# Mixer AB: ten taps of the Conformer convolution on TensorE instead of eight, fed by one more weight unit

## The chip, the cores and the metric

The kernel runs on one core of a Trainium2 chip. The metric is the device time of one execution in microseconds. The time before is 1874.81 us, the median of 3 runs (1874.71 to 1875.68).

## What is computed

The reference is a two-layer decoder trunk on a residual stream x of 512 tokens by 1024 features, in fp32. Each layer is a half-step SwiGLU FFN, a token mixer and another FFN, and every sub-layer is normalised before and after. The mixer of layer 0 is "AB". Its input projection gives four groups of 512 columns. Two of them feed the recurrent half (A), the other two the convolution half (B):

```python
z = h @ w_in
a_gate, a_x, b_val, b_gate = jnp.split(z, [W_A, 2 * W_A, 2 * W_A + W_B], axis=-1)
a_x = _causal_dwconv(a_x, a_conv_w, a_conv_b)                  # 4 taps
y_a = _rg_lru(a_x, a_gate_w, a_gate_b, a_lam) * jax.nn.gelu(a_gate)
v = b_val * jax.nn.sigmoid(b_gate)
v = _causal_dwconv(v, b_conv_w, b_conv_b)                      # 31 taps, one weight per channel and tap
v = layernorm of v over each of 8 groups of 64 channels
y_b = jax.nn.silu(v)
return jnp.concatenate([y_a, y_b], axis=-1) @ w_out
```

The change concerns the 31 taps of B's convolution: tap s adds v, shifted by s tokens and multiplied by one weight per channel, to the result.

## The kernel before

**Layout and precision.** Activations lie feature-major: a tile is 128 features by 512 tokens. Every fp32 matrix product is made from three TensorE passes over split operands (a rounded part and the rest, for weights and for activations): `mm3` (line 292) issues weight-high times data-high, weight-low times data-high and weight-high times data-low (lines 294 to 296).

**Phases.** FFN, mixer AB, FFN, FFN, mixer C, FFN follow each other, and the head of a phase overlaps the tail of the one before. During the first FFN a list of background jobs is run between its matmuls (`run_bg`, line 204): adaLN products, and for mixer AB `early` (line 683), which loads every weight unit of the mixer once, makes its low part (`split_w`, lines 280 and 281) and stores that to DRAM in `lows`.

**Mixer AB** (`rest`, line 931). The order of TensorE's units is written out in `ORDER` (line 31): "v t0 g x0 t1 x1 s0 t2 x2 s1 t3 x3 s2 a0 s3 a1 a2 a3". Here v and g are the last value and gate units of B, xj the inputs of A's recurrence, aj A's gate, sj the small gate products of the recurrence (lines 863 and 864, plain fp32), and tj the convolution taps of channel tile j. Then the output projection follows.

**The taps of tile j** go to three engines. TensorE takes the even shifts 0, 2, ..., 14 (NPE = 8) in `conv_pe` (line 759): each tap is a diagonal 128 by 128 weight and one `mm3` over 512 - 2i columns, all accumulated in one PSUM bank. Shift 1 is part of ScalarE's start value for GpSimd. `taps` (line 767) deals out the 22 other shifts: 11 (NPOOL) to GpSimd, for each of which ScalarE writes the product (line 784) and GpSimd adds it (line 785), and 11 to VectorE, which adds them into the PSUM bank that TensorE left (line 797). At line 802 VectorE joins both sums. Then `norm_b` (line 805) runs a chain between three engines: centring matmul (807), ScalarE (811, 813), group sums on TensorE (817), the reciprocal root on VectorE (325 to 335) and its copy (824), broadcast on TensorE (828), VectorE (833), ScalarE (836, 837), VectorE (839), ScalarE (842), VectorE (844).

**What sets the order of issue.** In this phase the instruction order of TensorE, ScalarE, VectorE and GpSimd is fixed by an issue clock kept in Python (`Flow`, line 226). Every `mm3` advances it by 3 times its columns over 2400. The side chains are generators that issue their next instruction once the clock has gone on by a constant: W_TAP = 0.9 after each VectorE tap, W_POOL = 1.404 after each GpSimd tap, W_N[0] = 0.5 between the last tap and line 802, W_N[1] = 4.0 between line 802 and the centring matmul. The queues of all engines are in order, so a side chain that runs late stops TensorE where its next matmul stands.

**Weight units.** `loads` (line 946) fetches each unit's 512 KB into one of four `raw` buffers (line 269, SyncE's queue), ScalarE makes the high part (line 953), and the low part comes back from `lows` (line 957). The units are taken in the order v, t0, g, x0 and so on. A unit tj holds eight diagonal weights, 1024 columns. v is split for the taps in `vsplit` (lines 926 and 928).

Of the kernel before, what the change touches and what calls it, by code (L numbers as in the profile page):

```python
# [7 lines left out]
F32 = mybir.dt.float32  # L8
F32R = mybir.dt.float32r
I32 = mybir.dt.int32  # L10
AF = mybir.ActivationFunctionType
# [3 lines left out]
P = 128  # L15
D = 1024
T = 512
KT = D // P
# [7 lines left out]

TMP, TMPH, CP = 4, 6, 2

NPE, NPOOL = 8, 11

ORDER = "v t0 g x0 t1 x1 s0 t2 x2 s1 t3 x3 s2 a0 s3 a1 a2 a3"
MANS = "PAVG"
# [50 lines left out]
def trunk_kernel(ctx: ExitStack, tc: tile.TileContext, a: dict, out: bass.AP):  # L83
    nc = tc.nc
    V, S, PE, G = nc.vector, nc.scalar, nc.tensor, nc.gpsimd
# [8 lines left out]
    def nm(base):  # L94
        uid[0] += 1
        return f"{base}_{uid[0]}"
# [9 lines left out]
    def t_hid(dt=F32):  # L106
        return sb.tile([P, T], dt, tag="hid", bufs=16, name=nm("hid"))
# [4 lines left out]
    def t_raw():  # L112
        return sb.tile([P, 1024], F32, tag="raw", bufs=4, name=nm("raw"))

    def t_mm(shape=(P, T)):
        return ps.tile(list(shape), F32, tag="mm", bufs=6, name=nm("mm"))
# [147 lines left out]
    def load_w(src, cols, eng=V):  # L264
        return split_w(fetch_w(src, cols), cols, eng)

    def fetch_w(src, cols):
        raw = t_raw()
        nc.sync.dma_start(raw[:, :cols], src)
        return raw  # L270

    def t_w():
        return (
            sb.tile([P, 1024], F32R, tag="wh", bufs=8, name=nm("wh")),
            sb.tile([P, 1024], F32R, tag="wl", bufs=8, name=nm("wl")),
        )
# [15 lines left out]
    def mm3(o, w, c0, hi, lo, start, stop, shared=False):  # L292
        wh, wl = w[0][:, c0 : c0 + P], w[1][:, c0 : c0 + P]
        PE.matmul(o, lhsT=wh, rhs=hi, start=start, stop=False, skip_group_check=shared)  # L294
        PE.matmul(o, lhsT=wl, rhs=hi, start=False, stop=False, skip_group_check=shared)  # L295
        PE.matmul(o, lhsT=wh, rhs=lo, start=False, stop=stop, skip_group_check=shared)  # L296
        flow.tick(3 * o.shape[1] / 2400)
# [176 lines left out]
    class PairHead(Ready):  # L474
# [6 lines left out]
        def fetch(self, k):  # L481
            self.raw[k] = fetch_w(self.src[k], 2 * self.n * P)
# [181 lines left out]
    lows = {}  # L664

    def low_jobs(srcs):
        def job(key, src, cols):
            wl = load_w(src, cols)[1]
            lows[key] = dram.tile([P, cols], F32, tag=nm("low"), name=nm("low"))
            later.append(lambda: nc.sync.dma_start(lows[key], wl.bitcast(F32)[:, :cols]))  # L670

        return [lambda v=v: job(*v) for v in srcs]


    class MixAB(Proj):
# [7 lines left out]
        def early(self):  # L683

            u = {"v": 0, "g": 1, **{f"x{j}": 2 + j for j in range(4)}, **{f"a{j}": 6 + j for j in range(4)}}
            src = lambda o: (a["ab_r"][u[o]], 1024) if o in u else (a["b_diag"][int(o[1])], NPE * P)
            units = [(o, *src(o)) for o in ORDER.split() if o[0] != "s"]
            return low_jobs(units + [(f"o{f}", self.wo[f], 1024) for f in range(KT)])

        def evac(self, j, val, gate, lo, hi):  # L690

# [67 lines left out]
        def conv_pe(self, j, w):  # L759
            vh, vl = self.vs[j][:, :T], self.vs[j][:, T:]  # L760
            o = t_mm()
            for i in range(NPE):
                c = T - 2 * i
                mm3(o[:, 2 * i :], w, i * P, vh[:, :c], vl[:, :c], i == 0, i == NPE - 1)
            self.ad[j] = o

        def taps(self):
# [163 lines left out]
        def rest(self):  # L931
# [3 lines left out]
            self.cv, self.ad, self.vs, self.x, self.y, self.sq = {}, {}, {}, {}, {}, set()  # L935

            r = lambda n: (a["ab_r"][n], 1024)
            d = lambda j: (a["b_diag"][j], NPE * P)
            unit_of = {"v": r(0), "g": r(1)}
            for j in range(4):  # L940
                unit_of[f"t{j}"], unit_of[f"x{j}"], unit_of[f"a{j}"] = d(j), r(2 + j), r(6 + j)
            order = ORDER.split()
            srcs = [(o, *unit_of[o]) for o in order if o in unit_of] + [(f"o{f}", self.wo[f], 1024) for f in range(KT)]
            ready = []

            def loads():
                while srcs:
                    while len(ready) > AHEAD:
                        yield 0.3
                    key, src, cols = srcs.pop(0)  # L950
                    raw = fetch_w(src, cols)
                    wh, wl = t_w()
                    S.activation(wh[:, :cols], raw[:, :cols], AF.Copy)
                    if len(ready) > 1:
                        yield 1.0
                    if key in lows:
                        nc.sync.dma_start(wl.bitcast(F32)[:, :cols], lows[key])
                    else:
                        V.tensor_tensor(
                            wl[:, :cols], raw[:, :cols], wh[:, :cols].bitcast(F32), op=SUB  # L960
                        )
                    ready.append((wh, wl))
                    if len(ready) > 1:
                        yield 1.0
# [4 lines left out]
            def wait(cond):  # L969
                while not cond():  # L970
                    flow.tick(0.2)

            def unit():
                wait(lambda: ready)
                return ready.pop(0)
# [5 lines left out]
                flow.start(self.gated(j, feat(None, unit())))  # L981

            def taps(j):
                wait(lambda: j in self.vs)
                self.conv_pe(j, unit())

            flow.tick(0)
# [281 lines left out]
    for n, ph in enumerate(phases):  # L1269
# [14 lines left out]
        with tc.manual_schedule(engines={nc.tensor.engine, nc.vector.engine}):  # L1284
            free = 8 - len(ph.wt)
            units = [] if last else list(range(KT))
# [128 lines left out]
```

## Time and profile before

| what | us |
|---|---|
| median of 3 runs | 1874.81 |
| the profiled execution, its own time | 1874.57 |
| its span, first to last instruction | 1872.4 |
| TensorE busy in the span | 1843.8 |
| VectorE busy | 1116.1 |
| ScalarE busy | 706.1 |
| GpSimd busy | 153.0 |

The span is what the instructions of the profiled execution cover; the remaining 2.17 us lie around it. Matmuls are pipelined, so that the busy time of a group of them counts overlaps twice; the start of the next one tells what one costs. The mixer's units v to a3 run from 429.46 to 543.54 us of the span.

### The profile page before, as it was taken

The page shows a single profiled execution, that of the slowest core. Times are in us where ns is not written, and L with a number is a line of the kernel's source. Part 1 is how long each engine was busy: PE and PEld are TensorE (multiplying, and loading weights), DVE is VectorE, ACT ScalarE, POOL GpSimd, SP SyncE. Part 2 cuts the span into 40 slices and gives each one's busy share as a digit, 9 for nine tenths or more (in the row PEclk, how much of TensorE's full clock was granted, in tenths as well). Part 3 has the DMA queues.
Part 4 walks back from the last instruction along what each step waited for, and adds up shares of the span by engine and source line. Part 5 has one row for each costly group of instructions (what it writes and reads, how often), then busy time and mean ns, then how long its engine had stood idle before and what let it go on. Part 6 is the DMA issues. An engine that isn't in the chain of part 4 may idle for free.

```text
span 1872.4 us, 25021 instructions
## 1 busy us (share of the span) xinstructions
PE 1843.8 (98%) x9636; PEld 1559.7 (83%) x9636; DVE 1116.1 (60%) x1967; ACT 706.1 (38%) x1058; POOL 153.0 (8%) x166
## 2 busy tenths in 40 slices
PE   9999999999799999999999999999999999999997
PEld 7788888998579888888898888888978998888887
DVE  7876767485856765455366665653675573344434
ACT  4444434246865433222234433232343342222221
POOL 0000000126512000000020000000300200000002
PEclk9999999999999999999999999999999999999999
DMA  8589889446355475564234996763433343334211
GB/s 330 183 306 309 317 315 315 131 163 222 135 203 169 163 272 190 162 222 153 92 119 167 318 310 217 278 237 103 158 101 119 119 127 112 118 94 134 90 45 46
DMA packets 103370, 344.76 MB, mean 184 GB/s; under 512 B 11473, under 2 KB 13649, under 8 KB 103250
## 3 DMA queue, kind: packets, MB, share of 16 engines
q1 hardware_dynamic: 103250, 343.16, 54.2%
q8 instruction: 76, 1.25, 0.3%
q14 instruction: 44, 0.36, 0.1%
HBM read 302.22 MB, written 40.89 MB: 183 GB/s over the span
## 4 chain that ended last, share of the span: by engine, by line
PE 92%; DVE 5%; ACT 2%; issue 1%; DMA 0%; POOL 0%; DVEq 0%; ACTq 0%; POOLq 0%
PE mm L296 29%; PE mm L294 29%; PE mm L295 29%; DVE ad L152 1%; PE st L345 1%; PE mm L1076 1%; PE mm L1078 1%; PE mm L1077 1%; PE st L355 1%; DVE mm L797 0%; PE mm L1129 0%; DVE y L408 0%; ACT tmp L1233 0%; ACT hh L1231 0%; DVE x L415 0%
## 5 line engine op out<-in xcount | busy, mean ns | idle before, releaser
L294 PE MATMUL mm<-hh,wh 128*128 128x512 f32 (+1 forms) x1728 | 641.7, 371 | 0.0
L296 PE MATMUL mm<-hl,wh 128*128 128x512 f32 (+1 forms) x1728 | 637.8, 369 | 0.1
L295 PE MATMUL mm<-hh,wl 128*128 128x512 f32 (+1 forms) x1728 | 636.3, 368 | 0.0
L280 ACT ACTIVATE wh<-raw 128x1024 fp32r<-128x1024 f32 (+2 forms) x324 | 328.1, 1016 | 528.4 <-PE mm L296 187.2
L281 DVE TENSOR_TENSOR wl<-raw,wh 128x1024 fp32r<-128x1024 f32 (+2 forms) x324 | 377.9, 1171 | 182.8 <-ACT wh L280 167.8
L296 PE MATMUL mm<-hid,wh 128*128 128x256 f32 (+1 forms) x1164 | 384.5, 330 | 0.0
L294 PE MATMUL mm<-hid,wh 128*128 128x256 f32 (+1 forms) x1164 | 384.0, 330 | 0.1
L295 PE MATMUL mm<-hid,wl 128*128 128x256 f32 (+1 forms) x1164 | 380.6, 327 | 0.0
L295 PEld LDWEIGHTS mm<-hh,wl 128*128 128x128 f32 x1728 | 325.3, 188 | 61.2 <-issue 1.7
L294 PEld LDWEIGHTS mm<-hh,wh 128*128 128x128 f32 x1728 | 325.0, 188 | 60.0 <-issue 2.0
L296 PEld LDWEIGHTS mm<-hl,wh 128*128 128x128 f32 x1728 | 325.0, 188 | 57.3 <-DVE hl L390 0.3
L295 PEld LDWEIGHTS mm<-hid,wl 128*128 128x128 f32 x1164 | 219.1, 188 | 23.7
L294 PEld LDWEIGHTS mm<-hid,wh 128*128 128x128 f32 x1164 | 218.5, 188 | 21.6 <-ACT hid L908 0.5
L296 PEld LDWEIGHTS mm<-hid,wh 128*128 128x128 f32 x1164 | 218.4, 188 | 21.4 <-DVE hid L910 0.4
L381 POOL TENSOR_TENSOR acc<-acc,tmph 128x256 f32<-128x256 f32 x112 | 90.5, 813 | 1651.2 <-ACT tmph L377 1649.3
L152 DVE SCALAR_TENSOR_TENSOR raw<-raw,cb 128x1024 f32<-128x1024 f32 x128 | 156.4, 1226 | 88.1 <-DMA raw<-in_ada_w_dram 87.8
L549 DVE SCALAR_TENSOR_TENSOR tmp<-tmp,mm 128x512 f32<-128x512 f32 x78 | 53.4, 685 | 112.4 <-PE mm L296 112.4
L594 DVE TENSOR_TENSOR y<-y,mm 128x256 f32<-128x256 f32 (+1 forms) x92 | 48.0, 523 | 116.2 <-PE mm L296 115.8
L548 DVE SCALAR_TENSOR_TENSOR tmp<-tmp,mm 128x512 f32<-128x512 f32 x78 | 53.4, 685 | 95.5 <-ACT tmp L547 95.2
L547 ACT ACTIVATE tmp<-mm 128x512 f32<-128x512 f32 x78 | 46.3, 593 | 164.7 <-PE mm L296 164.0
L377 ACT ACTIVATE tmph<-y 128x256 f32<-128x256 f32 x84 | 34.8, 416 | 105.3 <-DVE y L594 103.9
L286 ACT ACTIVATE hid<-tmp 128x512 fp32r<-128x512 f32 x87 | 54.0, 621 | 42.7 <-DVE tmp L549 31.0
(227 smaller groups left out, 1254.7 us busy)
## 6 DMA issues: line engine op xcount, KB each, us to landing
raw<-in_w13r_dram SPq DMA_DIRECT2D x150, 512.0 KB, 4.4
raw<-in_ada_w_dram SPq DMA_DIRECT2D x128, 512.0 KB, 4.6
raw<-in_w_dram SPq DMA_DIRECT2D x64, 448.0 KB, 4.2
raw<-in_w_dram SPq DMA_DIRECT2D x32, 512.0 KB, 3.5
raw<-in_w13h_dram SPq DMA_DIRECT2D x32, 384.0 KB, 4.3
kept<-wl SPq DMA_DIRECT2D x32, 384.0 KB, 3.4
wl<-kept SPq DMA_DIRECT2D x32, 384.0 KB, 3.4
low<-wl SPq DMA_DIRECT2D x22, 512.0 KB, 4.1
```

The costliest lines, as they stand in the source:

```text
L152: V.scalar_tensor_tensor(w, w, 0.5, cb, op0=MUL, op1=MUL, accum_out=modc[:, i : i + 1])
L280: S.activation(wh[:, :cols], raw[:, :cols], AF.Copy)
L281: eng.tensor_tensor(wl[:, :cols], raw[:, :cols], wh[:, :cols].bitcast(F32), op=SUB)
L286: S.activation(hi, src, AF.Copy)
L294: PE.matmul(o, lhsT=wh, rhs=hi, start=start, stop=False, skip_group_check=shared)
L295: PE.matmul(o, lhsT=wl, rhs=hi, start=False, stop=False, skip_group_check=shared)
L296: PE.matmul(o, lhsT=wh, rhs=lo, start=False, stop=stop, skip_group_check=shared)
L381: G.tensor_tensor(self.acc, self.acc, t, op=ADD)
L547: S.activation(t, g, AF.Tanh, scale=0.5)
L548: V.scalar_tensor_tensor(t, t, 1.0, g, op0=ADD, op1=MUL)
L549: V.scalar_tensor_tensor(t, t, 0.5, u, op0=MUL, op1=MUL)
L594: V.tensor_tensor(self.ys[f][:, lo:hi], self.ys[f][:, lo:hi], o, op=ADD)
```

## The change

NPE becomes 10: TensorE takes the shifts 0, 2, ..., 18. `taps` then has 20 other shifts to deal out, 11 to GpSimd as before and 9 to VectorE. A unit tj still holds eight diagonal weights. The two further ones of all four tiles (4 tiles by 2 taps by 128 columns, 1024 columns) come in one new unit "e": it is one more background job of `early`, and `loads` fetches it as the second unit, between v and t0, in runs of 1 KB per row and tile. Its high part is written by two ScalarE copies of 512 columns into two tiles of the `hid` pool, its low part comes by two transfers of 256 KB into two more, and the four stay until the taps of tile 3 are done. `conv_pe` waits, in issue order, for the unit to be there. No constant of the issue clock changes.

```diff
-NPE, NPOOL = 8, 11
+NPE, NPOOL = 10, 11
+
+NUNIT = 8
+NMORE = NPE - NUNIT
...
     def fetch_w(src, cols):
         raw = t_raw()
-        nc.sync.dma_start(raw[:, :cols], src)
+        dst = raw[:, :cols]
+        nc.sync.dma_start(dst if len(src.shape) == 2 else dst.rearrange("p (j c) -> p j c", j=src.shape[1]), src)
         return raw
+
+    def more_taps():
+        return a["b_diag"][:, :, NUNIT * P :].rearrange("j p c -> p j c")
...
-            src = lambda o: (a["ab_r"][u[o]], 1024) if o in u else (a["b_diag"][int(o[1])], NPE * P)
+            src = lambda o: (a["ab_r"][u[o]], 1024) if o in u else (a["b_diag"][int(o[1])][:, : NUNIT * P], NUNIT * P)
             units = [(o, *src(o)) for o in ORDER.split() if o[0] != "s"]
-            return low_jobs(units + [(f"o{f}", self.wo[f], 1024) for f in range(KT)])
+            return low_jobs(units + [("e", more_taps(), 4 * NMORE * P)] + [(f"o{f}", self.wo[f], 1024) for f in range(KT)])
...
             for i in range(NPE):
                 c = T - 2 * i
-                mm3(o[:, 2 * i :], w, i * P, vh[:, :c], vl[:, :c], i == 0, i == NPE - 1)
+                if i < NUNIT:
+                    u, c0 = w, i * P
+                else:
+                    k = j * NMORE + i - NUNIT
+                    u, c0 = self.more[k // 4], k % 4 * P
+                mm3(o[:, 2 * i :], u, c0, vh[:, :c], vl[:, :c], i == 0, i == NPE - 1)
             self.ad[j] = o
...
-            d = lambda j: (a["b_diag"][j], NPE * P)
+            d = lambda j: (a["b_diag"][j][:, : NUNIT * P], NUNIT * P)
...
-            srcs = [(o, *unit_of[o]) for o in order if o in unit_of] + [(f"o{f}", self.wo[f], 1024) for f in range(KT)]
+            unit_of["e"] = (more_taps(), 4 * NMORE * P)
+            self.more = None
+            srcs = [(o, *unit_of[o]) for o in ["v", "e"] + order[1:] if o in unit_of] + [(f"o{f}", self.wo[f], 1024) for f in range(KT)]
...
                     raw = fetch_w(src, cols)
+                    if key == "e":
+                        more = [(t_hid(F32R), t_hid(F32R)) for _ in range(2)]
+                        for i, (h, l) in enumerate(more):
+                            S.activation(h, raw[:, i * T : (i + 1) * T], AF.Copy)
+                            nc.sync.dma_start(l.bitcast(F32), lows[key][:, i * T : (i + 1) * T])
+                        self.more = more
+                        continue
...
             def taps(j):
-                wait(lambda: j in self.vs)
+                wait(lambda: j in self.vs and self.more)
                 self.conv_pe(j, unit())
```

## Rows read from the trace of the kernel before

**Rows 1.** The page, part 1: busy time and share of the span by engine.

```profile
PE 1843.8 (98%) x9636; PEld 1559.7 (83%) x9636; DVE 1116.1 (60%) x1967; ACT 706.1 (38%) x1058; POOL 153.0 (8%) x166
```

**Rows 2.** Windows: length, busy by engine (instructions), granted clock, DMA share, GB/s.

```profile
60.00:330.00 270.00, 269.28 (x1165) 217.93 (x1164) 195.89 (x292) 119.78 (x145) 0.00 (x0) 1.00 0.88 301
...
429.46:457.10 27.64, 27.64 (x123) 22.53 (x122) 14.96 (x22) 23.57 (x38) 21.67 (x17) 1.00 0.63 234
...
457.10:531.50 74.40, 60.78 (x250) 43.74 (x248) 62.78 (x120) 57.79 (x86) 36.40 (x28) 0.95 0.37 129
429.46:543.54 114.08, 100.47 (x426) 76.19 (x425) 86.95 (x154) 89.98 (x135) 58.07 (x44) 0.97 0.46 163
```

**Rows 3.** Waits of PE, 429 to 600 us: total us, times, longest.

```profile
PE st L828 <- DVE tmp L824: 6.9, 4, 3.1
PE st L807 <- DVE hid L802: 4.0, 2, 2.1
PE st L817 <- ACT tmp L811: 2.8, 3, 1.5
```

**Rows 4.** Windows around the slow clock, columns as in the group of windows above.

```profile
505.00:518.00 13.00, 9.94 (x33) 6.97 (x33) 11.65 (x25) 9.75 (x14) 6.47 (x4) 0.74 0.14 55
```

**Rows 5.** Chain that ended last, 440 to 545 us: shares by line.

```profile
by line: PE mm L296 9.7%; PE mm L295 9.7%; PE mm L294 9.6%; DVE mm L797 7.7%; POOL hid L785 4.7%; DMA raw<-in_ab_out_dram 4.4%; issue 4.0%; ACT wh L953 3.7%; DVE y L894 3.5%; DVE y L854 3.4%; PE st L828 3.0%; ACT cp L784 3.0%; DVE hid L844 
```

**Rows 6.** Timeline of PE in t0: start us, us, instruction.

```profile
435.01 0.40 PE L294 MATMUL mm<-vs,wh 128*128 128x512 f32 x1
...
438.01 0.39 PE L295 MATMUL mm<-vs,wl 128*128 128x504 f32 x1
...
440.50 0.39 PE L294 MATMUL mm<-hh,wh 128*128 128x512 f32 x1
```

**Rows 7.** Groups by line, 457.1 to 531.5 us: VectorE's taps of tiles 1 to 3.

```profile
L797 DVE SCALAR_TENSOR_TENSOR mm<-y,bw,mm 128x509 f32<-128x509 f32 (+10 forms) x33 | 24.1, 730 | 0.4
```

**Rows 8.** The page, part 5: the low part of a weight unit made on VectorE.

```profile
L281 DVE TENSOR_TENSOR wl<-raw,wh 128x1024 fp32r<-128x1024 f32 (+2 forms) x324 | 377.9, 1171 | 182.8 <-ACT wh L280 167.8
```

**Rows 9.** Timeline of SyncE's queue: start us, us, the fetches of t0 and g.

```profile
422.73 0.33 SPq L269 DMA_DIRECT2D raw<-in_b_diag_dram  x1
...
424.77 0.33 SPq L269 DMA_DIRECT2D raw<-in_ab_r_dram  x1
```

**Rows 10.** Windows at the mixer's start, columns as in the first group of windows.

```profile
425.00:430.00 5.00, 5.00 (x42) 4.91 (x41) 1.23 (x2) 2.20 (x3) 0.00 (x0) 1.00 0.96 347
```

**Rows 11.** Timeline of ACT before t0: start us, us, instruction, idle before it.

```profile
428.86 1.06 ACT L953 ACTIVATE wh<-raw 128x1024 fp32r<-128x1024 f32 x1 [1.40 <-DMA raw<-in_b_diag_dram]
...
430.68 0.63 ACT L926 ACTIVATE vs<-y 128x512 fp32r<-128x512 f32 x1 [0.21 <-DVE y L696]
```

**Rows 12.** Timeline of DVE: the split of v, the first root, the last join.

```profile
431.34 0.69 DVE L928 SCALAR_TENSOR_TENSOR vs<-y,vs 128x512 fp32r<-128x512 f32 x1 [0.37 <-ACT vs L926]
...
461.03 0.17 DVE L325 TENSOR_SCALAR sm<-st 128x8 f32<-128x8 f32 x1 [1.26 <-PE st L817]
...
522.22 0.68 DVE L802 TENSOR_TENSOR hid<-hid,mm 128x512 f32<-128x512 f32 x1
```

**Rows 13.** Timeline of PE: broadcasts of tiles 2 and 3, group sums of tile 3.

```profile
512.95 2.05 PE L828 MATMUL st<-ident,tmp 128*128 128x128 f32 x8 [3.06 <-DVE tmp L824]
...
526.98 1.05 PE L817 MATMUL st<-grp,tmp 128*128 128x2 f32 x8 [0.42 <-ACT tmp L811]
...
531.45 1.13 PE L828 MATMUL st<-ident,tmp 128*128 128x128 f32 x8 [1.22 <-DVE tmp L824]
```

**Rows 14.** Lines 844 and 824: count, duration ns min/median/max, first and last start.

```profile
L844 DVE SCALAR_TENSOR_TENSOR hid<-tmp,hid x4: 683/690/1719, 473.9 to 539.7; 128x512 fp32r<-128x512 f32 x4
...
L824 DVE COPY tmp<-sm x4: 426/710/1162, 463.7 to 530.9; 128x512 f32<-128x512 f32 x4
```

**Rows 15.** Timeline of POOL: the last nine taps of tile 0, the last of tile 3.

```profile
436.33 12.20 POOL L785 TENSOR_TENSOR hid<-hid,cp 128x499 f32<-128x499 f32 x9 [0.27 <-ACT cp L784]
...
518.04 1.23 POOL L785 TENSOR_TENSOR hid<-hid,cp 128x482 f32<-128x482 f32 x1 [2.53 <-ACT cp L784]
```

## The prediction

> **What bounds the kernel now.** I read the page first: TensorE is busy for 98% of the span [rows 1], so a change pays only where TensorE waits, and any matmul added elsewhere costs its full length. The windows tell where that is. In the first FFN TensorE is busy for 269.28 of 270 us. The mixer's units take 114.08 us, of which TensorE is busy for 100.47; that leaves 13.6 us idle. All of it lies behind the taps of tile 1: from 429.46 to 457.10 TensorE is busy throughout, from 457.10 to 531.50 for 60.78 of 74.40 us [rows 2]. The waits of TensorE name the three places, the same three in each tile's normalisation: the broadcast waits for VectorE's copy (6.9 us), the centring matmul for VectorE's join of both sums (4.0), the group sums for ScalarE (2.8). Together 13.7 us [rows 3]. There is a hidden loss beside them: between 505 and 518 us the granted clock averages 0.74, part of the stretch at 1.2 instead of 2.4 GHz, right where the longest waits have thinned TensorE's work [rows 4]. An average of 0.74 between 0.5 and 1 is 6.8 us at the low level; TensorE is busy 76% of this window and does half as much there, so about 2.6 us are lost (an estimate).
>
> What does TensorE wait for? In the 74.40 us VectorE is busy 62.78 us and ScalarE 57.79 [rows 2], neither of them full. The chain of waits through the mixer goes back and forth between VectorE, ScalarE and GpSimd; VectorE's taps have 7.7% of its 105 us, 8.1 us [rows 5]. So it is a chain through in-order queues with VectorE as its fullest member, not one saturated engine. TensorE is the bound up to 457 us, that chain from there to 531 us.
>
> **The change part by part.**
>
> *More matmuls.* Each tile gets two taps of three passes, 24 matmuls in all, over 496 and 494 columns. In t0, eleven matmuls of 504 to 498 columns take from 438.01 to 440.50 us, 0.226 us each [rows 6]. 24 × 0.225 = 5.4 us. Half of it, 2.7 us, falls in t0 and t1, where TensorE has no idle time [rows 2] and everything behind moves by as much; the other half falls in t2 and t3, between waits, and is paid only as far as these don't shrink. I count all 5.4 as cost and what shrinks as gain. The Trainium skill (TensorE: Matmul & The Clock Gate, "Back-to-back issue gap") has N/2.4 + 2.5 ns for one, 209 ns at 495 columns, so 5.0 us by the page; the row is 8% higher, and the row decides.
>
> *Fewer taps on VectorE.* With ten on TensorE, 20 shifts are left, 11 for GpSimd as before and 9 instead of 11 for VectorE: 8 instructions go, at 0.73 us each [rows 7], 5.8 us. Those of tile 0 lie before 457 us, where VectorE is busy 14.96 of 27.64 us [rows 2]: worth nothing. The six of tiles 1 to 3 take 4.4 us out of the chain that bounds.
>
> *The order of issue.* Nine taps advance the issue clock by 8.1 instead of 9.9, and two taps more on TensorE take 1.2 of it, so the normalisation of tile 0 is issued inside t1 instead of inside x1. In the trace its reciprocal root starts at 461.03 after VectorE sat idle for 1.26 us [rows 12]; with its centring done during t1 that idle time should go: a gain of 1.3 us, bounds 0 and 1.3.
>
> *The unit e in the first FFN.* One more job: a fetch of 512 KB, a split and a store of 512 KB. The subtraction is 1.17 us [rows 8], ScalarE's copy about as long. VectorE is busy 195.89 of 270 us there, ScalarE 119.78, the transfers 0.88 [rows 2]; 32 us of free transfer time cover 1 MB (3.5 us at that window's 301 GB/s). I take 0; without that cover some 1.2 us, the subtraction.
>
> *The unit e at the mixer's start.* This touches SyncE, the transfers, ScalarE and through it v's split. e takes the `raw` buffer that t0 had, and t0 the next one, that of g: 2.04 us later (422.73 to 424.77) [rows 9]. The transfers are 0.96 full at 347 GB/s then [rows 10], so that e's low half, if it is loaded there too, adds 1.5 us. ScalarE gets two copies of 512 columns before t0's, about 0.63 each by the copy of the same shape [rows 11], which fit into the wait for t0's data. Before, t0's high part started at 428.86, and behind it in the same queue v's split at 430.68 [rows 11]; VectorE finished that split at 431.34 + 0.69 = 432.03 [rows 12], and t0 starts on TensorE at 435.01 [rows 6]: 3.0 us of slack. A delay of 2.0 to 3.5 us costs t0 0 to 0.5 us. I take 0.3. At worst the 1 KB runs double the transfer (1.5 us more) and both copies come after it (1.3): 3.5 + 1.5 + 1.3 - 3.0 = 3.3 us. Lower end 0: nothing here can come earlier than before. Behind ScalarE stand also GpSimd's first products; GpSimd's taps of tile 0 end at 448.53 [rows 15], and TensorE waits for nothing of tile 0 before 457.10 [rows 2], so a start 2 to 3 us later is covered. The four `hid` tiles and the wait for unit e cost nothing in tile 1 and later, where the unit has long landed.
>
> *What comes back.* TensorE's removable loss is 13.7 + 2.6 = 16.3 us less what is pure latency. Tile 3 has no taps queued behind it and still shows 1.22 us before its broadcast and 0.42 before its group sums [rows 13]; four tiles of that are 6.5. So at most 9.8 us come back. The lower bound is what the taps had on the chain: 8.1 us for 44 taps, for 8 of them 1.5. I take the VectorE time that leaves the bounding chain, 4.4 + 1.3, and half of the clock loss, 1.3: 7.0 us.
>
> **The sum.** 5.4 + 0.3 - 7.0 = -1.3 us against the profiled execution's 1874.57 (span 1872.4 and 2.17 around it), 0.24 below the median: **1873.3 us**.
>
> A rule bears on the part that stays. The copy of line 824 has taken 426 ns at its shortest and 1162 at its longest, line 844 683 and 1719 [rows 14]; the short ones come after GpSimd's last tap at 518.04 [rows 15]. The Trainium skill (SBUF — State Buffer, "Who interferes with whom") says that a VectorE instruction with two SBUF inputs, or a copy in a two-port mode, contends with GpSimd, and one with at most one SBUF input doesn't. The removed taps read one operand from PSUM; by that rule they never paid it, and the stretched instructions keep paying, since GpSimd keeps its 44 taps. That speaks against a gain larger than the taps themselves.
>
> **The rivals.**
>
> *All waits fall to latency.* VectorE's relief and 2.7 us more cover in t2 and t3 take its lag away altogether, and with it the slow clock. For it: tile 2, which has the longest wait (3.06 us [rows 13]), is also where VectorE is fullest. Against it: ScalarE is nearly as busy and in the same chain. 5.4 - 9.8 = -4.4: 1870.2 us.
>
> *The waits move along (slower).* W_TAP and the 4.0 behind line 802 stay, so the centring matmul of a tile comes 1.8 units of the issue clock sooner behind its taps, while the recurrence's work on VectorE and the stretched instructions stay as they are. TensorE then meets the same late VectorE, only earlier in its own sequence, and the recurrence's scans pile up at tile 3 instead of tile 2. Only the chain share of the taps comes back: 5.4 + 0.3 - 1.5 = +4.2, 1878.8 us. It decides from the point where less than 5.7 us come back; it would show as waits at lines 807 and 828 of tile 3 that are not there now. For it: VectorE is on the chain for only part of the time [rows 5].
>
> *Unit e comes late.* t0 starts 3.3 us late: -1.3 + 3.0 = +1.7, 1876.3 us. For it the full transfers [rows 10], against it 3.0 us of slack.
>
> *The taps leave VectorE but GpSimd takes their place.* GpSimd's last tap ends at 519.27 [rows 15], and the last join starts at 522.22 [rows 12]: at that point VectorE can come only 2.9 us earlier before it waits for GpSimd. Then 5.4 + 0.3 - 2.9 = +2.8, 1877.4 us. Against it: half of GpSimd's tile 3 is itself held up by ScalarE, which the change relieves of nothing but waiting.
>
> **How the numbers follow.** A measurement of this kernel can tell about 0.2% from no change, 3.7 us: faster means below 1871.1, slower above 1878.5. Chances: the forecast 0.38, all waits to latency 0.27, the waits move 0.25, late e 0.06, GpSimd 0.04. The second lies mostly below 1871.1 (0.23), and a sixth of the forecast's spread as well (0.07): faster 0.30. Most of the third lies above 1878.5 (0.18), with small tails of the others (0.03): slower 0.21. The rest, 0.49, is within 0.2%. Faster and slower cases together hold over half, so the forecast's own range is worth giving: 1871 to 1876 us. The range of 8 in 10 reaches into both other cases, 1.2 us beyond each centre: 1869.0 to 1880.0.
>
> **What would show it.** Lines 294 to 296 with the taps' tile: 120 instead of 96 matmuls, t0 lasting 6.8 instead of 5.5 us. Line 797: 36 instead of 44. t0 starting within 0.5 us of the end of v. TensorE's three waits at 7 to 9 us instead of 13.7, and a granted clock of 0.85 or more in the stretch of tile 2. The mixer's units v to a3 at 112 to 114 us. I am wrong if the waits stay at 12 us or more (the third case, or GpSimd: then line 802 shows idle time of VectorE before it), if they fall to 6 and the clock stays up (the second), or if the time changes outside the mixer.

## The result and the profile after

The changed kernel takes **1886.29 us** (median of 4 runs, 1885.88 to 1887.11) against 1874.76 us for the kernel before on the same chip: ratio 1.0057, 95% interval [1.0046, 1.0069]. It is 11.5 us slower. The forecast of 1873.3 us is wrong, and its range, which ended at 1880.0, doesn't hold the time. The profiled execution took 1885.88 us with a span of 1884.1, 11.7 more than the span before.

The page of the changed kernel, part 1, answers to [rows 1]:

```profile
PE 1852.6 (98%) x9660; PEld 1566.3 (83%) x9660; DVE 1113.5 (59%) x1960; ACT 707.8 (38%) x1061; POOL 152.5 (8%) x166
```

TensorE has the 24 matmuls more. VectorE has the eight taps less and one split of a weight unit more, and is busy 2.6 us less. Both parts of the change are there. The windows of the changed kernel (columns as in [rows 2]) tell where the time is:

```profile
60.00:330.00 270.00, 269.23 (x1164) 217.89 (x1163) 195.43 (x293) 120.89 (x145) 0.00 (x0) 1.00 0.87 303
429.16:457.10 27.94, 27.94 (x123) 22.68 (x122) 13.42 (x20) 23.93 (x38) 21.61 (x17) 1.00 0.70 272
457.10:535.00 77.90, 63.85 (x249) 46.29 (x247) 57.62 (x100) 53.66 (x81) 35.97 (x28) 0.91 0.33 115
429.16:552.30 123.14, 108.51 (x451) 82.61 (x449) 82.37 (x144) 89.00 (x134) 57.57 (x44) 0.94 0.43 155
500.00:508.00 8.00, 3.84 (x14) 2.18 (x12) 5.90 (x8) 5.55 (x8) 4.01 (x4) 1.00 0.31 110
508.00:512.00 4.00, 3.13 (x11) 2.87 (x12) 4.00 (x3) 2.66 (x6) 3.26 (x4) 0.58 0.00 0
```

The first FFN is as before and TensorE is busy throughout up to 457.10, so neither the new weight unit nor t0 and t1 bring a wait. The mixer's units, v to a3, take 123.14 us instead of 114.08: 9.1 of the 11.7 us. Most of the rest lies at the start of the out-projection behind them, where TensorE waits 1.6 us. From there to the end of the last FFN its matmuls run 10.9 us behind those of the kernel before; the last 0.8 us lie behind them. VectorE is emptier than before, 57.62 us in 77.90 against 62.78 in 74.40. It was relieved, and the stretch that its chain was to shorten got longer.

The waits of TensorE in the changed kernel, from 425 to 600 us (total, times, longest). Lines move: the centring matmul 807 is now 819, the group sums 817 are 829, the broadcast 828 is 840, the gates 863 are 875:

```profile
PE st L840 <- DVE tmp L836: 7.4, 4, 2.8
PE st L829 <- ACT tmp L823: 4.5, 3, 3.3
PE st L819 <- DVE hid L814: 1.7, 1, 1.7
PE mm L301 <- ACT hid L920: 1.6, 1, 1.6
PE mm L875 <- DVE y L866: 1.0, 1, 1.0
```

Together 16.2 us, where [rows 3] has 13.7. The first three are the old waits, the last two are new. The granted clock is the second loss: the mean from 457 us to the last tile is 0.91 (0.95 before), and in 508 to 512 us it is 0.58, at 1.2 GHz for most of it, behind eight microseconds in which TensorE had been busy for 3.84. Summing TensorE's busy time times (1 - granted clock) over slices of 2 us from 426 to 600 us gives 3.1 us lost before and 6.1 after (an estimate).

So the profiled 11.7 us divide into **5.4 us of matmuls, 2.5 of waits and 3.0 of slow clock** (the last an estimate), 10.9 in all. In the timeline of TensorE the first three lines are t0's start, its last six matmuls' start and the next unit's start; below them stand the three waits at tile 2, one at the gates of tile 3 and one where the out-projection begins:

```profile
434.68 0.40 PE L301 MATMUL mm<-vs,wh 128*128 128x512 f32 x1
440.16 0.39 PE L301 MATMUL mm<-vs,hid 128*128 128x496 f32 x1
441.50 0.40 PE L301 MATMUL mm<-hh,wh 128*128 128x512 f32 x1
503.07 1.10 PE L819 MATMUL st<-hid,cen 128*128 128x512 f32 x2 [1.72 <-DVE hid L814]
508.87 1.86 PE L829 MATMUL st<-grp,tmp 128*128 128x2 f32 x8 [3.31 <-ACT tmp L823]
517.54 1.13 PE L840 MATMUL st<-ident,tmp 128*128 128x128 f32 x8 [2.76 <-DVE tmp L836]
529.32 1.10 PE L875 MATMUL mm<-y,hid 128*128 128x512 f32 x2 [1.00 <-DVE y L866]
556.73 0.50 PE L301 MATMUL mm<-hid,wh 128*128 128x512 f32 x1 [1.60 <-ACT hid L920]
```

Why do the group sums wait 3.31 us? ScalarE's timeline in the changed kernel shows what stands ahead of the square (line 823) that they need, although the centring matmul had been issued at 503.07:

```profile
502.42 0.72 ACT L895 ACTIVATE raw<-raw,ones 128x512 f32<-128x512 f32 x1 [2.77 <-DVE raw L893]
503.05 0.69 ACT L796 ACTIVATE cp<-y,bw 128x491 f32<-128x491 f32 x1
503.75 1.28 ACT L902 ACT_TABLE_LOAD   x1
505.05 1.15 ACT L902 ACTIVATE raw<-raw 128x512 f32<-128x512 f32 x2
506.11 0.69 ACT L796 ACTIVATE cp<-y,bw 128x489 f32<-128x489 f32 x1
506.70 1.04 ACT L974 ACTIVATE wh<-raw 128x1024 fp32r<-128x1024 f32 x1
507.65 0.69 ACT L796 ACTIVATE cp<-y,bw 128x487 f32<-128x487 f32 x1
508.24 0.57 ACT L823 ACTIVATE tmp<-st 128x512 f32<-128x512 f32 x1
```

The square roots of recurrences 0 and 1 (line 902), with a load of ScalarE's function table (1.28 us), a weight unit's copy and copies for GpSimd's taps, are issued ahead of it, and they come late, behind a wait of 2.77 us for VectorE. VectorE's queue goes on in the same way, the two scans ahead of tile 2's reciprocal root:

```profile
508.62 4.33 DVE L906 TENSOR_TENSOR_SCAN y<-raw 128x512 f32<-128x512 f32 x2
512.88 1.50 DVE L809 SCALAR_TENSOR_TENSOR mm<-y,bw,mm 128x505 f32<-128x505 f32 x2
514.28 0.16 DVE L332 TENSOR_SCALAR sm<-st 128x8 f32<-128x8 f32 x1
```

**Theory "order".** What costs is where the planner now puts the steps. The issue clock's constants (0.9 for a tap, 4.0 ahead of the centring, 2.0 ahead of the broadcast) were kept; two taps fewer on VectorE bring a tile's normalisation 1.8 units sooner, and two taps more on TensorE advance the clock by 1.2 within the tile. Counted in the traces without the added matmuls, the centring matmuls of the four tiles stand 9, 9, 12 and 6 matmuls earlier in TensorE's in-order queue and the broadcasts 15, 3, 6 and 6, that of tile 1 now ahead of the gates of recurrence 1 instead of behind them. Their inputs come hardly earlier: VectorE's joins of tiles 0 and 1 start at 454.43 and 478.33 us instead of 454.62 and 479.25. **Rivals:** the 24 matmuls or the new unit cost the time; or the taps' relief is worth nothing.

### The profile page after: what moved, and what is told of

Read it like the earlier page. It is cut to its first block, busy times and chain, and to the rows that moved or that the text cites. A ratio compares the mean times of both kernels' runs of the same rounds, so it can differ in the third digit from the quotient of the medians.

```text
span 1884.1 us, 25071 instructions
## 1 busy us (share of the span) xinstructions
PE 1852.6 (98%) x9660; PEld 1566.3 (83%) x9660; DVE 1113.5 (59%) x1960; ACT 707.8 (38%) x1061; POOL 152.5 (8%) x166
## 4 chain that ended last, share of the span: by engine, by line
PE 91%; DVE 5%; ACT 3%; issue 1%; POOL 0%; DMA 0%; DVEq 0%; ACTq 0%; POOLq 0%
PE mm L303 29%; PE mm L301 28%; PE mm L302 28%; DVE ad L155 1%; PE st L352 1%; PE mm L1097 1%; PE mm L1099 1%; PE mm L1098 1%; PE st L362 1%; PE mm L1150 0%; ACT wh L974 0%; DVE y L415 0%; ACT tmp L1254 0%; POOL hid L797 0%; ACT hh L1252 0%
```

## The experiments

All medians are of the runs of each kernel, ratios against the kernel before on the same chip; that kernel's median was 1875.9 to 1876.5 us there. A ratio is estimated from all the runs and isn't the quotient of two medians. What a run gives back of the change is told in medians from different chips; by the ratios it is the same within 0.3 us unless said.

**1 to 4. The parts by themselves.** The first has the whole change in the old order, its extra taps not advancing the clock and VectorE's nine taps in eleven slots:

```diff
...
-                mm3(o[:, 2 * i :], u, c0, vh[:, :c], vl[:, :c], i == 0, i == NPE - 1)
+                mm3(o[:, 2 * i :], u, c0, vh[:, :c], vl[:, :c], i == 0, i == NPE - 1, tick=i < NUNIT)
...
-                for s in self.taps()[1]:
+                for n in range(11):
+                    if n not in (3, 7):
+                        s = self.taps()[1][n - (n > 3) - (n > 7)]
...
```

> The whole change (ten taps on TensorE, nine on VectorE, unit e), but with the order of issue of the kernel before: the two further taps don't advance the issue clock, and VectorE's nine taps lie in the eleven slots of the kernel before, two of them empty. Theory O (the order that the clock now makes is what costs): the 11.5 us go, 1870 to 1876 us. Theory C (the matmuls and the unit cost by themselves, and the relief of VectorE is worth nothing): 1882 us or more.

The matmuls alone, in the kernel before:

```diff
...
-            for i in range(NPE):
+            for i in range(NPE + 2):
...
-                mm3(o[:, 2 * i :], w, i * P, vh[:, :c], vl[:, :c], i == 0, i == NPE - 1)
+                mm3(o[:, 2 * i :], w, i % NPE * P, vh[:, :c], vl[:, :c], i == 0, i == NPE + 1, tick=i < NPE)
```

> The kernel before with two more taps per tile on TensorE (weights of taps 0 and 1 once more, which adds terms that the convolution does not have), VectorE's eleven taps and the order of issue unchanged: the price of 24 matmuls alone. Theory O: what was predicted, 2.7 us in the dense stretch and up to 2.7 more between the waits, 1877 to 1881 us. Theory C: 1883 us or more.

VectorE's relief alone: the slots of run 1 and

```diff
-            rest = [s for s in range(2, 31) if s % 2 or s >= 2 * NPE]
+            rest = [s for s in range(2, 31) if s % 2 or s >= 2 * NPE + 4]
```

> The kernel before with nine taps per tile on VectorE in the eleven old slots, shifts 16 and 18 left out of the convolution, TensorE's eight taps and the order of issue unchanged: the relief alone. Theory O: 3 to 7 us faster, 1868 to 1872 us. Theory C: within 1.5 us of the kernel before, 1873 to 1876 us.

The unit alone: the change's fetch, split and wait, with the taps left at eight (one line of it):

```diff
...
-            srcs = [(o, *unit_of[o]) for o in order if o in unit_of] + [(f"o{f}", self.wo[f], 1024) for f in range(KT)]
+            srcs = [(o, *unit_of[o]) for o in ["v", "e"] + order[1:] if o in unit_of] + [(f"o{f}", self.wo[f], 1024) for f in range(KT)]
...
```

> The kernel before with unit e made in the first FFN and loaded as the second unit of the mixer, but not used: eight taps on TensorE, eleven on VectorE. Theory O: within 1.5 us of the kernel before, 1873.5 to 1876.5 us. Rival (the unit itself costs, by ScalarE's queue, the transfers or the four tiles it holds): 1878 us or more.

Measured: the change in the old order 1878.01 us, ratio 1.0007 [0.9997, 1.0017]; the matmuls alone 1878.76, 1.0013 [1.0004, 1.0022]; the relief alone 1874.87, 0.9996 [0.9986, 1.0005]; the unit alone 1875.46, 0.9996 [0.9986, 1.0005]. The waits of TensorE with the whole change in the old order:

```profile
PE st L843 <- DVE tmp L839: 6.7, 4, 2.9
PE st L832 <- ACT tmp L826: 2.5, 3, 1.4
PE st L822 <- DVE hid L817: 0.9, 2, 0.8
```

They are 10.1 us, 3.6 less than before. That isn't yet the worth of VectorE's relief: the unit alone takes nothing off VectorE, and its profiled execution waits 2.4 us less as well, as much less as that of the relief alone. The matmuls cost 2.8 us, the relief and the unit nothing that can be told from zero. Together the parts make 2.1 of the 11.5 us; the rest needs the new order.

**5 to 7. Which of the two shifts?** Run 5 has the second half of run 1's edit alone (the slots, 1.8 units), run 6 the first half alone (the ticks, 1.2), and run 7 gives the 1.8 back in the constant of the changed kernel:

```diff
-W_N = (0.5, 4.0, 0.2, 1.2, 0.3, 2.0, 0.3)
+W_N = (0.5, 5.8, 0.2, 1.2, 0.3, 2.0, 0.3)
```

> The whole change, its extra taps advance the issue clock as in the change, but VectorE's nine taps keep the eleven slots of the planner (slots 3 and 7 empty). So of the two things that moved the issue order, only the 1.8 units of the missing slots are given back, not the 1.2 that the extra taps tick. Theory 'slots' (nine slots bring the centring matmul 1.8 units too early): 1878 +- 2 us, waits of TensorE of 10 to 12 us. Theory 'ticks' (the extra taps' ticks pull work forward): 1884 us or more, waits of 15 us or more. If both share it: 1880 to 1883.

> The whole change with nine slots, but its extra taps do not advance the issue clock. Theory 'slots': stays at 1884 us or more with waits of 15 us or more. Theory 'ticks': 1878 +- 2 us. If both share it: 1880 to 1883.

> The change with one constant more: the 4.0 units of the issue clock ahead of the centring matmul become 5.8, which are the 1.8 units of the two slots that went. TensorE's order is then that of the run with nine taps in eleven slots. Theory 'slots': 1878 +- 2 us, within 2 us of that run. Theory 'ticks': 1884 us or more. A third theory, that the removed taps' own time was a cover for GpSimd's late partial sums: no better than the change, 1886 us.

Measured: 1876.11 us (0.9999 [0.9990, 1.0008]) with the slots kept, 1879.70 (1.0022 [1.0012, 1.0031]) without the ticks, 1877.87 (1.0006 [0.9997, 1.0016]) with the constant. Neither theory holds as put: undoing either shift brings most of the time back. With the 1.2 units of shift alone (run 5) the change is no slower than the kernel before, with the 1.8 alone (run 6) 3.7 us slower, with both 11.5. That isn't a sum; it would fit that what counts is beside which other step each one ends up.

**9. The new order without the new work.** The kernel before, with one constant:

```diff
-W_N = (0.5, 4.0, 0.2, 1.2, 0.3, 2.0, 0.3)
+W_N = (0.5, 1.0, 0.2, 1.2, 0.3, 2.0, 0.3)
```

> The kernel before, with its eight taps on TensorE and eleven on VectorE, and one constant changed: the 4.0 units ahead of the centring matmul become 1.0, the 3.0 units that the change has moved it up by. TensorE's order is then that of the changed kernel, less the 24 matmuls. Theory 'order': the time rises by 8 to 11 us with no work added or taken, to 1883 to 1887 us, tile 2's group sums wait 3 us or more for ScalarE, and the granted clock from 459 to 535 us falls to 0.92 or less. Theory 'interplay' (the order costs only together with the new work): it stays below 1880 us. The broadcast-later run made the first likelier, but nine slots alone (1879.7) and the ticks alone (1876.1) cost 3.7 and 0.1 us, so neither is sure.

Measured: **1887.13 us**, ratio 1.0058 [1.0042, 1.0073], the same ratio as the change. The waits of TensorE of that kernel (line numbers of before):

```profile
PE st L807 <- DVE hid L802: 13.6, 4, 6.4
PE st L828 <- DVE tmp L824: 3.6, 3, 1.9
PE mm L863 <- DVE y L854: 2.6, 1, 2.6
PE mm L294 <- ACT hid L908: 1.5, 1, 1.5
```

21.3 us of waits, and a granted clock of 0.88 from 459 to 535 us. With eleven taps on VectorE the early centring matmul meets the late join; with nine most of the delay is met one step later, at the square. Theory "order" is shown, by both halves together: with no matmul added and no tap taken an early order loses 11 us, and with the whole change in the old order (run 1) 2.1 are lost. The expectation erred in two things. Tile 2's group sums don't wait here, since the centring matmul takes the whole delay. And TensorE's order isn't quite that of the change: the steps of tiles 1 and 2 stand exactly there, but tile 0's centring is six matmuls earlier still and tile 3's three, with waits of 1.09 and 1.75 us that the change doesn't have. So the equal ratio is in part a coincidence, made of more waits and no added matmuls.

**10, 13, 14. Is it one meeting?** The first exchanges two neighbours of TensorE's queue at tile 1, the gates and the broadcast; the second lets the roots, products and scans of recurrences 0 and 1 go behind tile 2's steps on ScalarE and VectorE; the third moves the scans alone:

```diff
-                flow.start(self.norm_b(j), W_N[1])
+                flow.start(self.norm_b(j), W_N[1] + (0.6 if j == 2 else 0))
...
-            yield W_N[5]
+            yield W_N[5] + (1.0 if j == 1 else 0)
```

```diff
             V.scalar_tensor_tensor(t, t, 2.0, t, op0=SUB, op1=MUL)
-            yield 1.0
+            yield 1.0 + (4.4 if j == 1 else 0)
...
-            yield 0.6
+            yield 0.6 + (1.5 if j < 2 else 0)
             V.tensor_tensor_scan(x, r, t, 0.0, op0=MUL, op1=ADD)
```

(In the third the first of these two edits is left out and the 1.5 is 4.6. With the 0.6 of the first run tile 2's steps keep their place in TensorE's queue.)

> The whole change with one pair of steps of TensorE's order exchanged: the gates of recurrence 1 and the broadcast of tile 1, which in the change come in the order broadcast, gates and in the kernel before in the order gates, broadcast. Theory 'gates behind the broadcast': the wait of 2.17 us at the broadcast and its place hold up the gates, with them the square roots of recurrences 0 and 1, and behind these on ScalarE tile 2's centring; so this exchange alone gives back 4 us or more of the 10 (1882 us or less), and ScalarE's squares of tile 2 no longer stand behind the two square roots. Theory 'many small waits': it gives back no more than the 2.2 us of that wait, 1884 us or more.

> The whole change in its own order on TensorE, but recurrences 0 and 1 give way to tile 2's normalisation: their two square roots stand behind tile 2's squares on ScalarE, their last products and scans behind its reciprocal root and copy on VectorE. In the changed kernel ScalarE's square of tile 2 stands behind the two square roots (3.31 us of wait at the group sums), and the root behind the two scans (2.76 us at the broadcast). Theory 'meeting' (the 10 us of the order are made where the recurrences of tiles 0 and 1 meet tile 2's normalisation): both waits fall below 1 us and the slow clock between 508 and 525 us goes, 1878 us or less. Theory 'many small waits' (each step of each tile stands too early): only the two waits go, 1879 to 1882 us, and the waits of tiles 0 and 1 (6.2 us with tile 2's centring) stay.

> The whole change with the two scans alone behind tile 2's root and copy, the square roots where they were. As in the kernel before, where this move gave 3.6 us: the broadcast's wait of 2.76 us goes, and the time falls to 1882 to 1884 us. If the root is in truth held up by ScalarE's late square and not by the scans, it stays at 1885 to 1887 us.

Measured: 1883.78 us (1.0042 [1.0028, 1.0056]), 1882.24 (1.0037 [1.0023, 1.0051]) and 1886.87 (1.0061 [1.0048, 1.0075]). The exchange gave back 2.5 us: the wait of tile 1 is gone, but the square still starts behind the two roots. TensorE's timeline there:

```profile
505.90 1.43 PE L829 MATMUL st<-grp,tmp 128*128 128x2 f32 x8 [4.44 <-ACT tmp L823]
```

With roots and scans both later, tile 2's two waits fell to 0.85 and 0.53 us and the slow clock from 508 to 520 us was gone, as "meeting" asked, yet only 4.0 us came back: the clock is slow at other places instead, with 6.3 us lost in all (an estimate as above; 6.1 in the change). TensorE waits at the gates of tile 3 instead, which need VectorE's last step of `conv4`:

```profile
505.26 1.05 PE L829 MATMUL st<-grp,tmp 128*128 128x2 f32 x8 [0.85 <-ACT tmp L823]
509.05 1.13 PE L840 MATMUL st<-ident,tmp 128*128 128x128 f32 x8 [0.53 <-DVE tmp L836]
522.18 2.05 PE L875 MATMUL mm<-y,hid 128*128 128x512 f32 x2 [4.03 <-DVE y L866]
```

With the scans alone later nothing came back. The wait of 2.76 us at tile 2's broadcast is gone, and 2.5 us more appear at the same gates (1.00 in the change). So the time didn't stay because ScalarE held up the root, as that expectation had it, but because the wait moved:

```profile
514.64 1.41 PE L840 MATMUL st<-ident,tmp 128*128 128x128 f32 x8
527.55 1.10 PE L875 MATMUL mm<-y,hid 128*128 128x512 f32 x2 [3.51 <-DVE y L866]
```

So undoing the meeting at tile 2 gives back 4 us, with the new wait at tile 3's gates already paid out of it; the whole price of the meeting isn't shown.

Run 6 says more on the rest. In its trace TensorE's steps of tiles 2 and 3 stand exactly where the change has them; only tile 0's broadcast (six matmuls later) and tile 1's three steps (three to six later, the broadcast behind the gates) differ. Its largest waits are those of the group sums and of the broadcasts:

```profile
PE st L830 <- ACT tmp L824: 4.3, 2, 3.5
PE st L841 <- DVE tmp L837: 3.9, 4, 2.3
```

Its span is 5.8 us shorter than that of the change. The waits of tiles 0 and 1 are 3.4 us less there, those of tile 2 2.0 less, the rest equal. So half of what the change loses hangs on where the steps of tiles 0 and 1 stand, and 2 us of tile 2's waits go with it. That is told of TensorE's queue alone; the other engines' steps may have moved as well.

**8, 15, 16. Broadcasts later.** The old order with 3.6 instead of 2.0 ahead of the broadcast (first), the scans moved as well (second), and both on the kernel before (third):

```diff
-W_N = (0.5, 4.0, 0.2, 1.2, 0.3, 2.0, 0.3)
+W_N = (0.5, 4.0, 0.2, 1.2, 0.3, 3.6, 0.3)
```

> The whole change in the old issue order, and the 2.0 units of the issue clock ahead of the broadcast matmul become 3.6, since that matmul's wait for VectorE's copy was 6.7 of 10.1 us. Theory 'the waits are set by where in TensorE's order a matmul stands': this wait falls to 2 us or less, and the time to 1878.0 - 5 = 1873 us or below. Theory 'the chain is the bound, and a later place only moves the wait': the gates and the recurrence come later too, the waits appear at the next step or at the out-projection, and the time stays at 1877 to 1882 us.

> The whole change in the old order with the broadcasts later (1878.4 us, where one wait of 6.81 us at tile 2's broadcast took the place of four), and the scans behind tile 2's root and copy. Theory 'the scans make that wait': it falls by 4 us or more, and the time to 1872 to 1874 us. Rival 'a later place only moves the wait': 1876 us or more.

> The kernel before, eight taps on TensorE, with the broadcasts later and the scans behind tile 2's root and copy. With the scans alone it took 1872.6 us and still waited 3.8 us at broadcasts. If these waits go: 1869 to 1871 us. If the centring and group sums take them over: 1872 to 1874 us. Against the run before it in this list it tells what ten taps are worth where broadcasts wait for nothing: nearer than 1 us if the 5.4 us of matmuls and the relief of VectorE are even, 2 to 4 us faster if TensorE's time is all that counts there.

Measured: 1878.41 us (1.0012 [1.0003, 1.0022]), 1877.17 (1.0002 [0.9993, 1.0011]), 1874.77 (0.9996 [0.9987, 1.0005]). In the first, the broadcasts of the other tiles wait for nothing, and tile 2's takes the lot:

```profile
514.92 2.05 PE L843 MATMUL st<-ident,tmp 128*128 128x128 f32 x8 [6.81 <-DVE tmp L839]
```

In the second it is 5.51 us still, so the scans weren't most of it. Here a later place moves the wait; it doesn't end it. And where the broadcasts are later, eight taps beat ten by 2.4 us of the medians: nothing speaks there for the taps moved.

**11, 12. Only the scans later, in a good order.** The run with nine taps in eleven slots (5) with one edit, and the kernel before with the same:

```diff
-            yield 0.6
+            yield 0.6 + (4.6 if j < 2 else 0)
             V.tensor_tensor_scan(x, r, t, 0.0, op0=MUL, op1=ADD)
```

> The change with nine taps in eleven slots (1876.1 us), and the two scans of recurrences 0 and 1 issued on VectorE behind the reciprocal root and the copy of tile 2 instead of ahead of them; no other engine's order changes. In the kernel without this, the scans take 4.34 us at 503.29 and TensorE waits 3.28 us at tile 2's broadcast. Theory 'VectorE's scans make that wait': it falls below 0.5 us, the slow clock behind it goes too, and the time falls to 1871 to 1873 us, below the kernel before. Rival 'ScalarE and the chain make it': the wait stays above 2 us and the time at 1875 to 1877 us.

> The kernel before with the same move of the two scans alone. There the scans take 3.8 us from 503.83 and the broadcast of tile 2 waits 3.06 us. Theory 'VectorE's scans make that wait': 1870 to 1873 us. Rival: 1874 to 1877 us. Against the run before it in this list: if ten taps on TensorE are worth anything once the waits are gone, that one is the faster of the two; by 5.4 us of matmuls against 4.4 us of taps it should be the slower by 0 to 3 us.

Measured: 1873.40 us, 0.9985 [0.9976, 0.9993], and **1872.56 us, 0.9984 [0.9975, 0.9993]**; both are faster than the kernel before. The waits of TensorE in the first, with ten taps:

```profile
PE st L821 <- DVE hid L816: 2.5, 1, 2.5
PE mm L301 <- ACT hid L922: 1.4, 1, 1.4
PE st L842 <- ACT cp L796: 1.1, 1, 1.1
PE st L831 <- ACT tmp L825: 0.8, 2, 0.6
PE st L842 <- DVE tmp L838: 0.8, 2, 0.5
PE mm L877 <- ACT hid L856: 0.7, 1, 0.7
```

7.3 us, 6.4 less than before, and tile 2's broadcast waits for nothing. The kernel before with the same move still waits 12.2 us, does 5.4 us less on TensorE, and takes 0.8 us less, which the intervals don't tell from equal. In this order the two extra taps gain what they cost, and no more.

**The budget.** The same three terms, each against the kernel before, for the profiled execution of every run (waits summed as above, the clock estimated over the same slices; matmuls 24 × 0.225):

| run | matmuls | waits | clock | sum | span |
|---|---|---|---|---|---|
| the change | 5.4 | +2.5 | +3.0 | 10.9 | 11.7 |
| 1 old order | 5.4 | -3.6 | +3.3 | 5.1 | 5.5 |
| 2 matmuls only | 5.4 | -1.3 | +1.5 | 5.6 | 5.7 |
| 3 taps out only | 0 | -2.4 | +5.2 | 2.8 | 1.5 |
| 4 unit only | 0 | -2.4 | +1.5 | -0.9 | -1.3 |
| 5 slots kept | 5.4 | -4.5 | +1.7 | 2.6 | 1.9 |
| 6 no ticks | 5.4 | -2.9 | +2.3 | 4.8 | 5.9 |
| 7 norm later | 5.4 | -2.3 | +1.6 | 4.7 | 5.1 |
| 8 broadcasts later | 5.4 | -2.1 | +2.4 | 5.7 | 4.7 |
| 9 new order, old work | 0 | +7.6 | +5.6 | 13.2 | 12.6 |
| 10 gates first | 5.4 | -0.3 | +3.8 | 8.9 | 9.7 |
| 11 slots kept, scans later | 5.4 | -6.4 | +0.3 | -0.7 | -0.6 |
| 12 before, scans later | 0 | -1.5 | -1.4 | -2.9 | -2.3 |
| 13 roots and scans later | 5.4 | -0.7 | +3.2 | 7.9 | 7.9 |
| 14 scans later | 5.4 | +2.3 | +3.4 | 11.1 | 11.4 |
| 15 broadcasts and scans later | 5.4 | -3.3 | +1.4 | 3.5 | 3.0 |
| 16 before, both later | 0 | -2.6 | +3.6 | 1.0 | 0.9 |

The sums meet the spans within 1.3 us. A profiled execution can stand off its kernel's median (1 took 1879.70 there against 1878.01), and that of the kernel before, 1874.57, lies below its medians of 1875.9 to 1876.5 on the other chips, so that the differences of spans lean high. So the table explains spans, one execution each, and the ratios above give the sizes.

## Why the prediction was wrong

*More matmuls, +5.4.* Right. t0 runs from 434.68 to 441.50, 6.8 us as forecast, and its last six matmuls, from 440.16, take 1.34 us, 0.223 each. By the Trainium skill (TensorE: Matmul & The Clock Gate, "Back-to-back issue gap") it would be 0.209 at 495 columns, an estimate from its N/2.4 + 2.5 ns; the rows stay some 7% above it, and they decide. Alone the matmuls made 2.8 us of the medians in run 2. Its profiled execution has 5.7 us more span, with waits 1.3 us less and 1.5 us more lost to the clock; where the other half went in the median isn't shown.

*Fewer taps on VectorE.* The count (36, mean 733 ns) and with it the taps' own time are as forecast. What the relief is worth isn't: alone, in the old order, it gave a ratio of 0.9996 (run 3). That it can't shorten a chain whose steps wait in a queue for their turn would explain this, but no run shows it: run 3's waits did fall, by 2.4 us, and its loss to the clock rose.

*Unit e.* Right in both places: the FFN's window is unchanged, t0 starts 0.33 us earlier than in [rows 6], and the unit alone gave a ratio of 0.9996.

*The order of issue.* **This step failed.** It saw that tile 0's normalisation is issued sooner and asked only what that could gain, between 0 and 1.3 us, because VectorE had been idle ahead of the root. That idle time, which was to go, grew from 1.26 to 2.10 us, and the root came 1.1 us sooner while its broadcast stands 15 matmuls earlier:

```profile
459.94 0.17 DVE L332 TENSOR_SCALAR sm<-st 128x8 f32<-128x8 f32 x1 [2.10 <-PE st L829]
```

It didn't ask who stands behind the moved steps on TensorE. An early order with the old work costs 11 us in run 9, and undoing the order gives back 9.4 us of the change in run 1 (ratio 1.0057 to 1.0007).

*What comes back, -7.0.* Failed with it. Its lower bound of 1.5 us took for granted that existing waits can only shrink. In the old order they do, by 3.6 us, and by 6.4 in run 11; in the new one they grow by 2.5. And where half of the clock loss was to come back, 3.0 us more were lost (an estimate). The clock follows the waits loosely: in run 1 the waits fell by 3.6 and the clock still took 3.3.

*The rivals.* "The waits move along" was the right mechanism, at a chance of 0.25, with the right cause, the constants that stay. Its price was wrong. It was worked out from the share of the taps that comes back (+4.2 us), as if the waits would keep their size, and it left out the slow clock. Its sign, waits of tile 3 at centring and broadcast that weren't there, wasn't the one that came: the pile stayed at tile 2, and tile 3's gates and the out-projection got new waits. Of the signs put down, "waits of 12 us or more" decided rightly.

*The ports.* That VectorE's stretched instructions keep paying was right: the copy of line 836 took 427 to 1168 ns, like [rows 14]. The reading of the short ones was not quite: the copy at 512.37 us before took 0.43 us ahead of GpSimd's last tap, between two taps. What counts is whether a tap runs when the instruction starts. The two integer steps of the reciprocal root, which differ only in where they write, show it. The view of that one line has count, duration in ns (min/median/max) and first and last start:

```profile
L334 DVE TENSOR_SCALAR st<-sm x4: 170/170/172, 460.1 to 536.3; 128x8 int32<-128x8 int32 x4
L334 DVE TENSOR_SCALAR sm<-sm x4: 163/740/1152, 460.2 to 536.4; 128x8 int32<-128x8 int32 x4
```

The one from SBUF to PSUM takes 170 ns (min, median, max alike), the one within SBUF up to 1152 ns. It is stretched in three tiles of four (0.75, 1.15 and 0.73 us), each time from its start within a GpSimd tap to 0.03 us behind that tap's end, as at tile 1:

```profile
485.40 1.24 POOL L797 TENSOR_TENSOR hid<-hid,cp 128x483 f32<-128x483 f32 x1
485.51 1.15 DVE L334 TENSOR_SCALAR sm<-sm 128x8 int32<-128x8 int32 x1
```

In the kernel before it was stretched in one tile (0.70). At its tile 1 it started at 484.79, between a tap's end at 484.75 and the next one's start at 484.83, and took 0.16 us. In the traces of all the runs, where a tap has more than 0.16 us left at its start, it ends 0.03 us behind that tap; elsewhere it takes 0.16 us. One to three tiles of a kernel are hit, in either order of issue. The Trainium skill (SBUF — State Buffer, "Who interferes with whom") says that a copy or `tensor_scalar` can run in a two-port mode, and that it then contends with GpSimd, where the one that comes second blocks fully; the times in the traces agree, while in which mode these instructions ran they don't show. The three cost 2.1 us of a chain that TensorE waits for, 1.6 more than in the kernel before.

## What to carry to other kernels

Where the order of in-order queues is made by hand-set costs, a change of work is also a change of order, and the order can be worth more than the work: test it by moving the constants with the work held fixed, and the work with the order held fixed. When a step is moved ahead, ask of each engine's queue what it is now in front of, and whether its inputs come sooner too; a bound of zero for a loss needs a reason. And a wait on a fully loaded TensorE can be paid twice, as itself and in the slow clock behind it: here 2.5 and 3.0 us more.

## What was not expected of the hardware

The slow clock's share of the differences is as large as that of the waits, and it doesn't go in step with them. With two taps simply left out (run 3) the waits of the profiled execution fell by 2.4 us and the loss to the clock rose by 5.2, at two places. Where the waits were few (run 11) TensorE still ran with a mean granted clock of 0.66 over ten microseconds, behind a wait of 2.48 us ahead of the centring matmul at 501.43:

```profile
500.00:510.00 10.00, 8.57 (x24) 6.49 (x25) 8.99 (x21) 6.25 (x11) 5.14 (x5) 0.66 0.01 2
```

And one wait, of 1.9 us ahead of tile 0's broadcast, has a slow clock behind it in the change (0.72 on the mean from 463.5 to 469.5 us) and none in run 13 (1.00), where it is the same; in the kernel before a wait of 1.81 us there has none either. Which waits bring it and which don't stays open; no run here separates them. Executions of one kernel differ too (run 12 took 1872.1 to 1874.4 us), so that one profiled execution of each can't settle it.
